# Attention weights turned by VectorE blocks and DMA instead of TensorE, weighted sums one head later, scores in two PSUM pools

## The chip, the cores and the metric

The kernel runs on one core of one Trainium2 chip. The metric is the device time of one execution in microseconds. Three runs of the kernel before took 1411.1, 1411.3 and 1412.79 us; the median is 1411.3 us. TensorE multiplies matrices into PSUM (eight banks here: three for projections, five for everything else), VectorE and ScalarE do elementwise work, reductions and activations, GpSimd some elementwise work, and SyncE issues nearly all DMAs on one queue, in order.

## The reference

One step of a two-layer encoder trunk in fp32, on 512 prompt tokens and 32 sample tokens of width 1024. Layer 0 mixes tokens by RWKV-7 and is not touched. Layer 1 is differential attention with 12 heads of width 128 (each query and key split into two halves of 64), beside four memory heads; everything is multiplied by a SiLU gate, projected out and added to the input.

```python
mask = k_pos[None, :] < (q_pos[:, None] // CHUNK + 1) * CHUNK
def probs(qa, ka):
    s = jnp.einsum('bqhd,bkhd->bhqk', qa, ka).astype(jnp.float32) * DF_HD ** -0.5
    return jax.nn.softmax(jnp.where(mask, s, NEG_INF), axis=-1)
attn = probs(q1, k1) - lam * probs(q2, k2)
return jnp.einsum('bhqk,bkhd->bqhd', attn.astype(v_all.dtype), v_all)
...
o = rmsnorm(o, subln) * (1.0 - lam_init)
out = jnp.concatenate([o.reshape(B, T, MIX_W), y_mem], axis=-1) * jax.nn.silu(gate)
```

The keys and values of layer 1 are outputs too (512 prompt and 32 sample rows, 12 heads).

## The kernel before

**Projections.** Activations lie transposed in SBUF, 128 features by 544 tokens, eight such tiles, each split into a high and a low part (hh, hl). A projection of 128 columns (gemm, line 341, called by proj, line 357) is 2 halves of 272 tokens × 8 tiles × 3 products = 48 matmuls into a PSUM tile called ps_g. Its weights come as two DMAs of 256 KB into raw (load, line 274), and ScalarE and VectorE split them into whi and wlo (split, line 303). There are five raw tiles and two pairs whi/wlo; used (line 293) splits the next block and issues the load of a later one.

**Layer 1** (layer1, line 1649) runs diff_group (line 1734) for three groups of four heads. For each head it projects v, k and q. The helper turned (line 1768) transposes v and k in 32×32 blocks on VectorE (tile kv) and writes them with four DMAs in runs of 128 bytes to a DRAM tile scr, from which vt (values by token) is read back and, at the end of the group, the outputs are copied. The high parts of k lie on half of the partitions of kh; a DMA kh<-kh copies each half to the other partitions, so that scores of both halves can be made with a correction kz.

**Attention of a head** is a loop over four query tiles t of 128 tokens, with n = 128 (t + 1) keys. For both maps, two matmuls give the scores in a PSUM tile ps_s of pool psc, which has two banks; VectorE sets the masked corner and takes the row maximum, ScalarE takes the exponential with its sum (softmax, line 1080), and VectorE forms the difference of both maps in pt (combine, line 1882). TensorE transposes the n columns of pt into ps_aT (pool psm, two banks), ScalarE copies them to aT, TensorE multiplies with vt into ps_o (pool psx, one bank), VectorE copies to ot and ScalarE takes the sum of squares.

**End of a group.** The same is done once for the sample tokens of four heads (tiles ssb, ps_saT, ps_os, os, ps_osT). Then rsqrt (line 124, nine small VectorE steps) gives the norms; for each head four scalings of ot, four transposes into ps_oT, a gate projection (gate, line 952, into one of two tiles sg) and two VectorE products into og follow. Groups 0 and 1 are followed by two memory heads each. In group 2, four of the sixteen og tiles are split ahead (early). After it comes the output projection (w_out, line 1226), which takes the heads of group 2 last.

**What sets the order.** In layer 1 nothing is ordered by hand. When the program is built, each engine's instructions are put in a fixed order: among those that the builder reckons ready, the one that stands first in the source goes first. On the chip each engine takes its instructions in that order and waits where one isn't ready. So TensorE's scores stand between matmuls of the next head's projections, and DMAs stand in SyncE's queue in the order that the builder reckoned.

Line 105 in the profile is the helper that issues every recorded operation, so rows are told apart by tile names.

Of the kernel before, what the change touches and what calls it, by code (L numbers as in the profile page):

```python
# [9 lines left out]
F32 = mybir.dt.float32  # L10
# [23 lines left out]
QB, KB, KVB = 2, 1, 2  # L34
# [73 lines left out]
class Trunk:  # L108
# [823 lines left out]
    def gate_evac(self, n):  # L932
        nc = self.nc
        sg = self.sg[n % SGB]

        def evac(ps, v):
            self.ae.activation(sg[:, v], ps, AF.Tanh, scale=0.5)
            gated = lambda: self.ve.scalar_tensor_tensor(sg[:, v], sg[:, v], 1.0, ps, ALU.add, ALU.mult)
            if not self.ordered:
                return gated()  # L940
            done.append(self.put_off(gated, 0.43))
            return gated

        done = []

        def get():
            self.until(done[-1])
            return sg

        return sg, get, evac  # L950

    def gate(self, src, c0):

        self.gates += 1
        sg, _, evac = self.gate_evac(self.gates)
        self.proj(src, c0, evac)
        return sg
# [136 lines left out]
    def mem_head(self, i, h, w, cq, cg, p):  # L1094

        st = {}
        it = self.mem_steps(st, i, h, p)
        for _ in range(3):
            next(it)
        st["q"], evac = self.query_evac(p)  # L1100
        self.proj(w, cq + h * P, evac)
        for _ in range(9):
            next(it)
        sg = self.gate(w, cg + h * P)
        st["gate"] = lambda: sg
        for _ in it:
            pass
# [207 lines left out]
    def layer0(self, mem):  # L1315
# [6 lines left out]
        with ExitStack() as ctx:  # L1322
# [45 lines left out]
            def add_gate(pr, st, c0, n):  # L1368
                def make(wt):
                    sg, st["gate"], evac = self.gate_evac(n)  # L1370
# [278 lines left out]
    def layer1(self):  # L1649
# [4 lines left out]
        with ExitStack() as ctx:  # L1654
            made, order = {}, list(range(8)) + [12, 13, 14, 15, 8, 9, 10, 11]
            with ExitStack() as c2:
# [9 lines left out]
                early = None  # L1666
                for hg in range(3):
                    self.diff_group(hg, w, p, self.ls[:, 2:3], early)
# [9 lines left out]
        with ExitStack() as ctx:  # L1678
# [36 lines left out]
            def consume(k, ps, v):  # L1715
                x = self.x1[:, k, v]
                self.ve.tensor_tensor(x, ps, x, ALU.add)
                self.square_sums((k, x, v), p, sums)
                if k == 3 and v.start:
# [14 lines left out]
    def diff_group(self, hg, w, p, nlam, early):  # L1734
# [9 lines left out]
        vs = p.tile([TS, 4, P], F32, tag="vs", name="vs")  # L1744
        scr = [self.dp.tile([T, 4, P], F32, tag=f"scr{i}", name=f"scr{i}", bufs=2) for i in range(2)]
        ssb = p.tile([P, 2, 160], F32, tag="ssb", name="ssb")
        on = []
        ss = p.tile([P, 3, 16], F32, tag="oss", name="oss")
        for j in range(4):
# [27 lines left out]
            vt = p.tile([P, 4, P], F32, tag="vt", name="vt", bufs=2)  # L1777
            self.se.dma_start(vt[:], scr[1][:TP, j, :].rearrange("(i p) d -> p i d", p=P))
# [6 lines left out]
            turned(0, k)  # L1785
            self.proj(w, h * P, q_parts)
            self.ae.copy(ks[:, j, :], k[:, TP:])
            if j == 1:
# [3 lines left out]
                self.ae.copy(ckT[:], ps[:].rearrange("p (j c) -> p j c", j=4))  # L1792
            if j == 3:
# [3 lines left out]
            ot = p.tile([P, 4, P], F32, tag="ot", name="ot", bufs=4)  # L1797
            on.append(ot)
# [23 lines left out]
        self.se.dma_start(vs[:], scr[1][TP:])  # L1822
# [9 lines left out]
        aT = p.tile([P, 512], F32, tag="aT", name="aTs", bufs=2)  # L1832
# [7 lines left out]
        for j in range(4):  # L1840
            rj = slice(32 * j, 32 * j + 32)
            self.te.matmul(po[rj, :P], aT[:TS, P + 32 * j : P + 32 * j + 32], vs[:, j, :], start=False, stop=True,
# [4 lines left out]
        jk = p.tile([P, P], F32, tag="jk", name="jks", bufs=2)  # L1847
# [7 lines left out]
        self.ae.activation(oT[:], psT[:, :P], AF.Copy, scale=self.subs)  # L1855
        self.ve.tensor_scalar(ss[:, 1, :], ss[:, 0, :], 1.0 / P, EPS, ALU.mult, ALU.add)
        self.rsqrt(ss[:, 2, :], ss[:, 1, :], p, "nt16")
        for j in range(4):
# [8 lines left out]
            self.ve.tensor_tensor(g[:, TP:], oT[:, 32 * j : 32 * j + 32], sg[:, TP:], ALU.mult)  # L1867

# [20 lines left out]
    def run(self):  # L1889
# [18 lines left out]
        self.sg, self.gates = [gp.tile([P, T], F32, name=f"sg{i}") for i in range(SGB)], 0  # L1908
# [54 lines left out]
```

## Time and profile before

| | |
|---|---|
| median of three runs | 1411.3 us |
| profiled execution, its own time | 1410.51 us |
| its span | 1408.8 us |
| granted TensorE clock, mean | 0.993 |
| busy: TensorE, weight loads | 1357.8, 1286.3 us |
| busy: VectorE, ScalarE, GpSimd | 915.3, 810.5, 423.3 us |
| DMA: packets, data | 315734, 151.07 MB |

Every row of a view names the source line, the engine (PE is TensorE, PEld its weight loads, DVE VectorE, ACT ScalarE, POOL GpSimd, SPq SyncE's queue), the operation, and output<-inputs by tile name with buffer numbers left out. In a group, "x120 | 21.3, 276 | 0.7" means 120 instructions, 21.3 us busy, 276 ns mean, and 0.7 us of idle time of that engine ahead of them, with what ended it. In a timeline a row gives start, duration and the number of instructions merged. Matmuls overlap, so a duration of 0.29 us can go with a start every 0.126 us. A row of waits reads: who waited <- for whom: total us, times, longest.

### The profile page before, as it was taken

What the parts mean: (1) busy time and instruction counts of PE and PEld (TensorE: products, weight loads), DVE (VectorE), ACT (ScalarE), POOL (GpSimd) and SP (SyncE); (2) the same over time, 40 slices, a digit from 0 to 9 for tenths busy, and PEclk for the clock granted to TensorE, in tenths of its full rate; (3) what the DMA queues carried; (4) which work ended last, traced back from release to release, by engine and by line L of the source; (5) the groups of instructions that cost most, each with busy time, mean ns of one, the idle gap of its engine ahead of it and who ended that gap; (6) DMA issues with size and microseconds to landing.
All of it is one profiled execution on the core that took longest, in us unless ns stands there. A gap on an engine that the chain in (4) does not pass through costs nothing.

```text
span 1408.8 us, 31764 instructions
## 1 busy us (share of the span) xinstructions
PE 1357.8 (96%) x11762; PEld 1286.3 (91%) x11762; DVE 915.3 (65%) x2352; ACT 810.5 (58%) x2239; POOL 423.3 (30%) x874
## 2 busy tenths in 40 slices
PE   6998999999999999899999999999999999999997
PEld 6998889999999999798899999999999999999996
DVE  7765777787778787665754566674465746568443
ACT  7665677767777777565533366554465445555321
POOL 2226576566856586520120040000001001110000
PEclk9999999999999999999999999999999999999998
DMA  7542223333233222333464474452444424453321
GB/s 241 176 136 59 62 62 83 84 75 78 63 84 90 68 65 75 90 89 105 136 191 126 139 216 109 100 157 83 114 99 112 145 75 103 102 140 119 105 68 64
DMA packets 315734, 151.07 MB, mean 107 GB/s; under 512 B 112361, under 2 KB 300018, under 8 KB 315578
## 3 DMA queue, kind: packets, MB, share of 16 engines
q1 hardware_dynamic: 315434, 148.50, 38.2%
q8 instruction: 93, 1.52, 0.4%
q14 instruction: 63, 0.52, 0.1%
q10 hardware_dynamic: 144, 0.52, 0.1%
HBM read 120.62 MB, written 31.69 MB: 108 GB/s over the span
## 4 chain that ended last, share of the span: by engine, by line
PE 45%; DVE 2%; ACT 1%; DMA 1%; issue 1%; DVEq 0%; ACTq 0%
PE ps_g L105 36%; PE ps_o L105 2%; PE ps_s L105 2%; PE ps_aT L105 1%; DVE wlo L105 1%; PE ps_mm L105 1%; DVE qp L105 1%; DMA kh<-kh 1%; PE ps_mo L105 1%; ACT whi L105 1%; PE ps_oT L105 0%; PE ps_mt L105 0%; ACT pt L105 0%; PE ps_f L105 0%; DVE snm L105 0%
## 5 line engine op out<-in xcount | busy, mean ns | idle before, releaser
L105 PE MATMUL ps_g<-hh,whi 128*128 128x272 f32 x1808 | 540.3, 299 | 0.9 <-ACT hh L105 0.9
L105 PE MATMUL ps_g<-hh,wlo 128*128 128x272 f32 x1808 | 539.2, 298 | 1.2 <-DVE wlo L105 1.2
L105 PE MATMUL ps_g<-hl,whi 128*128 128x272 f32 x1808 | 533.3, 295 | 0.6 <-POOL hl L477 0.5
L105 PEld LDWEIGHTS ps_g<-hh,whi 128*128 128x128 f32 x1808 | 343.7, 190 | 6.2 <-ACT hh L105 1.3
L105 PEld LDWEIGHTS ps_g<-hh,wlo 128*128 128x128 f32 x1808 | 343.1, 190 | 5.1 <-DVE wlo L105 2.0
L105 PEld LDWEIGHTS ps_g<-hl,whi 128*128 128x128 f32 x1808 | 342.9, 190 | 3.5 <-POOL hl L477 0.7
L105 DVE TENSOR_TENSOR wlo<-raw,whi 128x512 fp32r<-128x512 f32 x322 | 228.8, 722 | 165.8 <-ACT whi L105 164.0
L105 ACT CAST whi<-raw 128x512 fp32r<-128x512 f32 x322 | 194.5, 617 | 158.9 <-PE ps_g L105 129.6
L766 POOL TENSOR_TENSOR tm<-u,m 102x84 f32<-102x84 f32 (+23 forms) x372 | 154.6, 415 | 167.3 <-DMA m<-sc 139.1
L768 POOL TENSOR_TENSOR u<-u,tm 102x84 f32<-102x84 f32 (+23 forms) x372 | 162.9, 438 | 29.1
L105 PE MATMUL ps_g<-lo,whi 128*128 128x272 f32 x512 | 147.9, 289 | 0.7 <-DVE lo L105 0.7
L105 PE MATMUL ps_g<-hi,wlo 128*128 128x272 f32 x512 | 147.8, 289 | 0.0
L105 PE MATMUL ps_g<-hi,whi 128*128 128x272 f32 x512 | 147.7, 288 | 0.0
L1784 POOL TENSOR_TENSOR kz<-k,kh 64x544 fp32r<-64x544 f32 x24 | 37.0, 1540 | 318.8 <-ACT kh L105 317.9
L105 PEld LDWEIGHTS ps_g<-lo,whi 128*128 128x128 f32 x512 | 96.5, 188 | 1.1 <-DVE lo L105 1.1
L105 PEld LDWEIGHTS ps_g<-hi,whi 128*128 128x128 f32 x512 | 96.6, 189 | 0.0
L105 PEld LDWEIGHTS ps_g<-hi,wlo 128*128 128x128 f32 x512 | 96.5, 189 | 0.0
L105 DVE SCALAR_TENSOR_TENSOR SB<-ps_c,dl,sd 64x64 f32<-64x64 f32 x168 | 47.4, 282 | 44.0 <-PE ps_c L105 38.2
L105 ACT COPY sv<-ps_c 64x64 f32<-64x64 f32 x192 | 39.2, 204 | 38.2 <-PE ps_c L105 36.4
L105 ACT ACTIVATE pt<-ps_s,snm 128x128 f32<-128x128 f32 (+3 forms) x96 | 50.9, 531 | 15.0 <-DVE snm L105 14.2
L105 ACT ACTIVATE sg<-ps_g 128x272 f32<-128x272 f32 x64 | 25.2, 394 | 42.4 <-PE ps_g L105 40.0
L105 DVE TENSOR_REDUCE snm<-ps_s 128x1 f32<-128x128 f32 (+3 forms) x96 | 46.1, 485 | 1.0
(367 smaller groups left out, 2496.1 us busy)
## 6 DMA issues: line engine op xcount, KB each, us to landing
raw<-in_rw_in_dram SPq DMA_DIRECT2D x114, 256.0 KB
raw<-in_df_in_dram SPq DMA_DIRECT2D x112, 256.0 KB
raw<-in_w_out_dram SPq DMA_DIRECT2D x64, 256.0 KB
scr<-kv SPq DMA_DIRECT2D x96, 68.0 KB
out_dram<-scr SPq DMA_DIRECT2D x6, 1024.0 KB
m<-sc SPq DMA_DIRECT2D x36, 128.0 KB
oscr<-sg SPq DMA_DIRECT2D x16, 272.0 KB
lo<-oscr SPq DMA_DIRECT2D x16, 272.0 KB
```

Source lines behind the costliest of these rows:

```text
L105: return lambda *a, **k: self.trunk.tie(self, issue(*a, **k))
L766: nc.gpsimd.tensor_tensor(tm[:, :n, :wd], u3[:, :n, kx : kx + 1].to_broadcast(sh), m3[:, kx : kx + 1, kx + 1 :].to_broadcast(sh), ALU.mult)
L768: nc.gpsimd.tensor_tensor(u3[:, :n, kx + 1 :], u3[:, :n, kx + 1 :], tm[:, :n, :wd], ALU.add)
L1784: nc.gpsimd.tensor_tensor(kz[rows[m], m, :], k[rows[m], :], hi.bitcast(F32), ALU.subtract)
```

## The change

The attention weights are no longer transposed on TensorE. After combine, VectorE transposes pt in 32×32 blocks into a tile pk, which holds all ten 128×128 parts of a head (40 × 32 columns; one buffer). When the head's four query tiles are done, four DMAs write pk in runs of 128 bytes to a DRAM tile ptr (two buffers). The read of ptr into aT, now one tile for all ten parts (one buffer), stands in the source behind the next head's q projection. The weighted sums of all four query tiles stand behind the next head's softmax; they go into the four quarters of one PSUM bank, with one copy to ot and then four sums of squares. For the fourth head of a group, the read stands behind the second of the four gate projections and the sums behind the fourth.

The four gate projections of a group now stand together ahead of the norms, and each writes into its head's tile og, in which the product is formed in place. The two sg tiles serve as the buffers of turned. Scores of query tiles 1 and 3 go to pool psm, those of 0 and 2 to psc. The read of vt stands behind the writes of k. The copies of keys and values to the outputs (kv_out) move from the end of a group to the third head of the next, and for the last group into the output projection. The new rows of the sample's values use ck's buffer.

```diff
+        def weighted(j, ptr, vt):
+            aT = p.tile([P, 10, P], F32, tag="aT", name="aT", bufs=1)
+            self.se.dma_start(aT[:], ptr[:].rearrange("(i b) t c -> (b t) i c", b=4))
+            yield
+            ot = p.tile([P, 4, P], F32, tag="ot", name="ot", bufs=4)
+            on.append(ot)
+            po = self.psx.tile([P, 4, P], F32, tag="x", name="ps_o")
+            for t in range(4):
+                i0 = t * (t + 1) // 2
+                for i in range(t + 1):
+                    self.te.matmul(po[:, t, :], aT[:, i0 + i, :], vt[:, i, :], start=i == 0, stop=i == t)
+            self.ve.tensor_copy(ot[:], po[:])
+            for t in range(4):
+                jk = p.tile([P, P], F32, tag="jk", name="jk", bufs=1)
+                self.ae.activation(jk[:], ot[:, t, :], AF.Square, accum_out=ss[:, 0, 4 * j + t : 4 * j + t + 1])
...
             def turned(i, x):
-                kv = p.tile([P, T // 32, 32], F32, tag="kv", name="kv", bufs=KVB)
-                self.ve.transpose(kv[:].rearrange("p b c -> p (b c)"), x[:])
+                kv = self.sg[i][:].rearrange("p (b c) -> p b c", c=32)
+                self.ve.transpose(self.sg[i][:], x[:])
...
             turned(1, v)
-            vt = p.tile([P, 4, P], F32, tag="vt", name="vt", bufs=2)
-            self.se.dma_start(vt[:], scr[1][:TP, j, :].rearrange("(i p) d -> p i d", p=P))
...
             turned(0, k)
+            vt = p.tile([P, 4, P], F32, tag="vt", name="vt", bufs=2)
+            self.se.dma_start(vt[:], scr[1][:TP, j, :].rearrange("(i p) d -> p i d", p=P))
             self.proj(w, h * P, q_parts)
+            if late:
+                next(late)
...
+            if j == 2:
+                before()
...
-                    ps = self.psc.tile([P, 512], F32, tag="c", name="ps_s")
+                    q, g = (self.psm, "m") if t % 2 else (self.psc, "c")
+                    ps = q.tile([P, 512], F32, tag=g, name="ps_s")
...
                 self.combine(pt, rs, n, nlam)
-                ps = self.psm.tile([P, 512], F32, tag="m", name="ps_aT")
-                for i in range(t + 1):
-                    self.te.transpose(ps[:, i * P : i * P + P], pt[:, 0, i * P : i * P + P], self.ident[:])
-                aT = p.tile([P, 512], F32, tag="aT", name="aT", bufs=2)
-                self.ae.copy(aT[:, :n], ps[:, :n])
-                po = self.psx.tile([P, 512], F32, tag="x", name="ps_o")
-                for i in range(t + 1):
-                    self.te.matmul(po[:, :P], aT[:, i * P : i * P + P], vt[:, i, :], start=i == 0, stop=i == t)
-                self.ve.tensor_copy(ot[:, t, :], po[:, :P])
-                jk = p.tile([P, P], F32, tag="jk", name="jk", bufs=2)
-                self.ae.activation(jk[:], ot[:, t, :], AF.Square, accum_out=ss[:, 0, 4 * j + t : 4 * j + t + 1])
+                b0 = 2 * t * (t + 1)
+                self.ve.transpose(pk[:, b0 : b0 + 4 * (t + 1)].rearrange("p b c -> p (b c)"), pt[:, 0, :n])
+            if late:
+                next(late, None)
+            ptr = self.dp.tile([40, 32, P], F32, tag="ptr", name="ptr", bufs=2)
+            for b in range(4):
+                self.se.dma_start(ptr[:, :, 32 * b : 32 * b + 32].rearrange("n t c -> t n c"), pk[32 * b : 32 * b + 32])
+            late = weighted(j, ptr, vt)
...
-        for i in range(2):
-            self.se.dma_start(o[4 + i][0, 0, :, 4 * hg : 4 * hg + 4, :], scr[i][:TP])
-            self.se.dma_start(o[10 + i][0, 0, :, 4 * hg : 4 * hg + 4, :], scr[i][TP:])
+        def kv_out():
+            for i in range(2):
+                self.se.dma_start(o[4 + i][0, 0, :, 4 * hg : 4 * hg + 4, :], scr[i][:TP])
+                self.se.dma_start(o[10 + i][0, 0, :, 4 * hg : 4 * hg + 4, :], scr[i][TP:])
...
+        sgs = []
+        for i, g in enumerate(range(4 * hg, 4 * hg + 4)):
+            sgs.append(self.gate(w, 3 * MIXW + 512 + g * P, g))
+            if i == 1:
+                next(late)
+        next(late, None)
         self.ve.tensor_scalar(ss[:, 1, :], ss[:, 0, :], 1.0 / P, EPS, ALU.mult, ALU.add)
...
-            sg = self.gate(w, 3 * MIXW + 512 + (4 * hg + j) * P)
-            g = self.dest(4 * hg + j, sg)
+            g = sg = sgs[j]
```

More of the change, by code (lines that the diff above doesn't have):

```diff
@@ L33 @@
 KAPPA = 0.5 * math.exp(-0.5)
-QB, KB, KVB = 2, 1, 2
+QB, KB, PKB = 2, 1, 1
 RKV = 4
@@ L950, in gate_evac, with gate @@
         return sg, get, evac
-    def gate(self, src, c0):
-        self.gates += 1
-        sg, _, evac = self.gate_evac(self.gates)
+    def gate(self, src, c0, g):
+        sg, _, evac = self.gate_evac(self.o1[g])
         self.proj(src, c0, evac)
@@ L1103, in mem_head @@
             next(it)
-        sg = self.gate(w, cg + h * P)
+        sg = self.gate(w, cg + h * P, 12 + h)
         st["gate"] = lambda: sg
@@ L1666, in layer1 @@
                 early = None
+                kv_out = lambda: None
                 for hg in range(3):
-                    self.diff_group(hg, w, p, self.ls[:, 2:3], early)
+                    kv_out = self.diff_group(hg, w, p, self.ls[:, 2:3], early, kv_out)
                     for h in ((0, 1), (2, 3), ())[hg]:
@@ L1718, in consume @@
                 self.square_sums((k, x, v), p, sums)
+                if k == 2 and not v.start:
+                    kv_out()
                 if k == 3 and v.start:
@@ L1732, in layer1, with diff_group @@
                 pass
-    def diff_group(self, hg, w, p, nlam, early):
+    def diff_group(self, hg, w, p, nlam, early, before):
         nc, a, o = self.nc, self.a, self.o
@@ L1743, in diff_group @@
         ks = p.tile([P, 4, TS], F32, tag="ks", name="ks")
-        vs = p.tile([TS, 4, P], F32, tag="vs", name="vs")
         scr = [self.dp.tile([T, 4, P], F32, tag=f"scr{i}", name=f"scr{i}", bufs=2) for i in range(2)]
         ssb = p.tile([P, 2, 160], F32, tag="ssb", name="ssb")
-        on = []
+        on, late = [], None
+        def weighted(j, ptr, vt):
[13 more added lines that the diff above has]
+                self.ae.activation(jk[:], ot[:, t, :], AF.Square, accum_out=ss[:, 0, 4 * j + t : 4 * j + t + 1])
         ss = p.tile([P, 3, 16], F32, tag="oss", name="oss")
@@ L1841, in diff_group @@
             rj = slice(32 * j, 32 * j + 32)
-            self.te.matmul(po[rj, :P], aT[:TS, P + 32 * j : P + 32 * j + 32], vs[:, j, :], start=False, stop=True,
+            self.te.matmul(po[rj, :P], aT[:TS, P + 32 * j : P + 32 * j + 32], vs[:TS, j, :], start=False, stop=True,
                              tile_position=(0, 32 * j))
@@ L1907, in run @@
         gp = self.pool("gate", 1)
-        self.sg, self.gates = [gp.tile([P, T], F32, name=f"sg{i}") for i in range(SGB)], 0
+        self.sg = [gp.tile([P, T], F32, name=f"sg{i}") for i in range(SGB)]
         self.rctx = ExitStack()
```

16 lines of the change are left out of this document (8 added, 8 removed).

## The prediction

> **What bounds the kernel now.** I read the page first (engines, chain), then the busy time of the stage that the change touches, then TensorE's own waits in it, and last the order of instructions around one head.
>
> ```profile
> span 1408.8 us, 31764 instructions
> PE 1357.8 (96%) x11762; PEld 1286.3 (91%) x11762; DVE 915.3 (65%) x2352; ACT 810.5 (58%) x2239; POOL 423.3 (30%) x874
> PE 45%; DVE 2%; ACT 1%; DMA 1%; issue 1%; DVEq 0%; ACTq 0%
> ```
>
> The page: TensorE is busy nearly throughout and has by far the largest share of the chain that ended last. The change lies in the differential attention, from 833 us (first DMA of a turned head) to 1283 us. The table of stretches (columns: PE, PEld, DVE, ACT, POOL busy, granted clock, DMA share, GB/s) and TensorE's waits there:
>
> ```profile
> 833.00:1283.00 450.00, 444.37 (x3415) 417.38 (x3415) 267.65 (x793) 241.59 (x715) 40.62 (x26) 1.00 0.43 115
> 858.00:861.00 3.00, 3.00 (x25) 2.91 (x26) 1.86 (x5) 0.79 (x3) 0.00 (x0) 1.00 0.98 231
> 861.00:866.00 5.00, 5.00 (x41) 4.80 (x40) 1.42 (x3) 2.77 (x7) 0.00 (x0) 1.00 0.14 22
> PE ps_s L105 <- ACT pt L105: 3.5, 7, 0.6
> PE ps_s L105 <- DMA kh<-kh: 0.6, 2, 0.3
> ```
>
> TensorE is busy 444.4 of 450 us, and its two kinds of wait shown are 3.5 and 0.6 us in total; VectorE is at 59%, ScalarE at 54%, the DMA engines at 43%. While a softmax runs, TensorE multiplies the next head's projection, so this stage lasts as long as TensorE's instructions take. Whatever leaves TensorE there comes off the time, as long as no new wait appears. Because matmuls overlap, their durations say too much; I price by the distance between starts.
>
> **The change part by part.**
>
> *The transposes of the weights leave TensorE* (10 per head, 120 in all, in runs of 1 to 4). One run in order of time, with the projection's matmuls (ps_g) around it, and the plain rate of ps_g from the chain:
>
> ```profile
> 860.34 0.29 PE L105 MATMUL ps_g<-hl,whi 128*128 128x272 f32 x1
> 860.53 0.63 PE L105 MATMUL ps_aT<-ident,pt 128*128 128x128 f32 x4
> 860.91 0.37 PE L105 MATMUL ps_g<-hh,wlo 128*128 128x272 f32 x1
> 861.12 0.29 PE L105 MATMUL ps_g<-hh,whi 128*128 128x272 f32 x1
> ...
> 889.12 7.42 PE ps_g L105 x59
> ```
>
> 59 matmuls in 7.42 us are 0.126 each. From the start of the ps_g ahead of the run to the start of the second ps_g behind it, less these two: 861.12 − 860.34 − 2 × 0.126 = 0.53 us for four, 0.13 each with the switch between kinds of matmul inside. I take shorter runs in proportion: 1.33 us a head, **15.9 us** in all.
>
> *The weighted sums stay, but in one run per head instead of four.* They appear as two passes each:
>
> ```profile
> 854.65 0.28 PE L105 MATMUL ps_g<-hl,whi 128*128 128x272 f32 x1
> 854.89 0.71 PE L105 MATMUL ps_o<-vt,aT 128*128 128x128 f32 x4
> 855.36 0.37 PE L105 MATMUL ps_g<-hh,wlo 128*128 128x272 f32 x1
> 855.57 0.29 PE L105 MATMUL ps_g<-hh,whi 128*128 128x272 f32 x1
> ...
> 861.62 0.29 PE L105 MATMUL ps_g<-hl,whi 128*128 128x272 f32 x1
> 861.89 1.16 PE L105 MATMUL ps_o<-vt,aT 128*128 128x128 f32 x8
> 862.80 0.37 PE L105 MATMUL ps_g<-hh,wlo 128*128 128x272 f32 x1
> 863.01 0.29 PE L105 MATMUL ps_g<-hh,whi 128*128 128x272 f32 x1
> ```
>
> Four passes cost 0.92 − 0.25 = 0.67 us, eight 1.39 − 0.25 = 1.14: 0.118 a pass and 0.20 per run. Three runs fewer per head save 0.6 us, **7.2 us** in all; at worst (each 0.20 is a wait for aT that comes back in another form) nothing.
>
> *Scores in two pools.* The 3.5 us of ps_s on the exponentials above are the wait for one of two score banks. With four banks I take them as gone: **3.5 us**, between 0 and 3.5. Four banks may also join score matmuls into fewer runs; at 0.20 per run, as for ps_o, that is up to 48 × 0.2 = 9.6 us more, of which I count none.
>
> *What the new path puts on VectorE and ScalarE.* Rows by form in this stage:
>
> ```profile
> L105 DVE COPY ot<-ps_o 128x128 f32<-128x128 f32 x48 | 13.9, 289 | 30.8 <-PE ps_o L105 30.6
> L105 DVE STREAM_TRANSPOSE kv<-k 128x544 f32<-128x544 f32 x12 | 8.9, 738 | 0.0
> L105 DVE TENSOR_SCALAR ot<-ot,oss 128x128 f32<-128x128 f32 x32 | 7.7, 281 | 0.0
> ```
>
> Block transposes: 1280 columns per head at 738/544 = 1.36 ns are 1.74 us, 20.8 us in all. Out go the 13.9 us of ot copies; in come 12 wider ones (at most four old ones, 1.16 us each). So VectorE gets 7 to 21 us more on 267.65 of 450, ScalarE loses its copies of aT. Neither sets the end: VectorE's share stays under 70%, so both fit under TensorE's matmuls. A block transpose needs pk free, that is the last head's writes landed; behind it on VectorE stand the next softmax and the splits of weights (wlo) that TensorE needs. A head lies between, so I price this at nothing. VectorE also stops waiting 30.6 us for ps_o in the middle of its queue, which lets a softmax end up to 2.5 us earlier.
>
> *What it puts on the DMA engines.* Per head four writes with 40 × 32 × 4 = 5120 runs of 128 bytes and one read with 1280 runs of 512 bytes. Two looks at the DMA queue, 858 to 862 us and 884 to 888 us, have different mixes:
>
> ```profile
> DMA packets 3296, 0.80 MB, mean 201 GB/s; under 512 B 2272, under 2 KB 3296, under 8 KB 3296
> q1 hardware_dynamic: 3296, 0.80, 90.4%
> ...
> DMA packets 2887, 0.60 MB, mean 150 GB/s; under 512 B 2256, under 2 KB 2887, under 8 KB 2887
> q1 hardware_dynamic: 2887, 0.60, 73.0%
> ```
>
> In engine time: 2272 s + 1024 b = 0.904 × 64 us = 57.9 and 2256 s + 631 b = 46.7, so b = 28 ns and s = 13 ns. The writes are 5120 × 13/16 = 4.2 us of all engines, the read 2.2: 6.4 per head, 77 us in all on 0.43 × 450 = 194. A share of about 63% still fits. The traffic moved later (the copies of k and v to the outputs) is the same amount.
>
> *Two new places where TensorE can wait.* All of this goes on SyncE's one queue, in order:
>
> ```profile
> 858.41 2.33 SPq L105 DMA_DIRECT2D scr<-kv  x4
> 865.59 0.39 SPq L105 DMA_DIRECT2D raw<-in_df_in_dram  x1
> 866.22 1.13 SPq L105 DMA_DIRECT2D kh<-kh  x2
> 867.52 0.45 SPq L105 DMA_DIRECT2D vt<-scr  x1
> ...
> 866.22 4.73 DMA kh<-kh
> ```
>
> The writes wait for the last block transpose, the read waits for the writes and for the last head's ps_o; behind them in the queue stand the raw loads and kh<-kh. First, the read of aT, which ps_o waits for. Its nearest relative is vt, read back from what scr<-kv wrote. In the source vt stands ahead of the k projection; in the fixed order it was put behind kh, which needs the whole k projection. The writes had left the queue by 861 us (share 0.14 from then on), so that order reckons with a round trip of 6 us or more where the chip took about 3. An order that is too careful places ps_o after aT is there. I take 0 us; one microsecond too early per head makes 12, and the next head's v projection stands behind it.
>
> Second, kh<-kh, the swap that the next head's scores need. It is in the chain with 4.73 us and has no margin: the second of the wait rows above shows TensorE already waiting for it. A softmax of head 0 is over at 860.5 (its transposes start at 860.53), kh goes out at 866.22: 5.7 us. TensorE's savings take 2.1 us from this gap, the last block transpose 0.7, the quicker softmax gives back up to 2.5; so 2.9 to 5.4 us for a burst of 4.2. The wait is 0 to 1.3 us for each of 11 heads; I take 0.3, what the longest such wait measures now: **+3.3 us**.
>
> *Gates, sample path, tail.* The four gates are the same matmuls into other tiles, and stand now as cover over the sample's softmax. Behind them come the last head's sums, 16 scalings (16 × 0.281 = 4.5 us) and the squares and small steps ahead of them; I put this at 11 us. Cover: the memory heads after groups 0 and 1; after group 2 the output projection's six part products that don't need these heads, 144 × 0.126 = 18 us. Cost 0 to 3 us, once; I take **+1**. Without that cover it would be 11.
>
> Sum: −15.9 − 7.2 − 3.5 + 3.3 + 1.0 = −22.3 us. The profiled execution took 1410.5 us (its span 1408.8 and 1.7 around it) and would take 1388.2; it stands 0.8 under the median of 1411.3, so against the median the forecast is **1389 us**. Bounds: with no new wait −26.6 (1385); with sums in one run worth nothing, score waits unchanged, kh at 1.3 us a head and the tail at 3: −15.9 + 14.3 + 3 = +1.4 (1413).
>
> **The rivals.**
>
> *The swap stands behind the weights (slower).* If the four writes go out right ahead of kh<-kh, what is left of the 4.2 us burst delays every head's scores, and TensorE, which takes its instructions in order, waits. It decides at 26.6/11 = 2.4 us a head, more than half the burst. With three quarters left (3.2 us): 1411.3 − 26.6 + 35 = 1420. For it: no margin for kh, a queue at 98% during such writes. Against: the gap of 2.9 to 5.4 us.
>
> *Sums too early.* ps_o is put where aT isn't there yet, 1 us per head: 1389 + 12 = 1401. For it: two DRAM trips in a row, one aT buffer. Against: the place of vt.
>
> *No change.* Savings and waits cancel, for instance because weights (raw) queue behind 77 us more of DMA: 1411. Against: no row in which TensorE waits for raw.
>
> *Scattered writes are far dearer than scr's.* In a stage of 428 us, with 194 us of other traffic and 26 of reads, 208 us stay for 61,440 runs, 3840 per engine: 54 ns each, four times the 13 measured. At six times, 300 us, the stage lasts 520 and the kernel 1389 + 92 = 1481. Packets of the same form in scr<-kv speak against it. The Trainium skill ("VectorE: DVE Perf Modes", The three transpose paths) warns that a plain DMA copy doing a transpose by strides is 19× slower than the crossbar one, and its table for kernel authors sends a 128×128 transpose to TensorE. By that rule this change would be a loss; the trace disagrees for this shape, since the blocks are turned on VectorE and runs of 128 bytes stay whole at 13 ns.
>
> **How the numbers follow.** Forecast (1384 to 1396): 0.54. Better than that, by score matmuls in fewer runs (about 1381): 0.10. Sums too early or half the gain eaten (about 1401): 0.14. No change: 0.07. Swap behind the weights: 0.13. Dear writes: 0.02. The range 1380 to 1410 leaves out the last two cases, part of no change and little of the better one. A measurement of this kernel tells 0.2%, 2.8 us, from no change: faster 0.78, same 0.07, slower 0.15.
>
> **What would show it.** Right: no ps_aT, TensorE's starts as dense as now, ps_o in runs of 20 passes, the stage some 22 us shorter (450 to 428), rows of TensorE waiting for aT or kh under 5 us. Wrong: a row "PE ps_s <- DMA kh" or "PEld ps_o <- DMA aT" with more than 1 us a head, ps_g's starts spread by late weights, or a hole at the start of the output projection.

## The result and the profile after

The changed kernel takes 1474.3 us (median of four runs, 1473.3 to 1476.9) against 1411.2 us before (four runs): ratio 1.045, 95% interval 1.043 to 1.047. It is 63 us slower where 22 us less were forecast. The page of the changed kernel, its first two lines, and its table of stretches (columns as in the prediction), first changed, then before:

```profile
span 1473.0 us, 31439 instructions
PE 1374.1 (93%) x11642; PEld 1298.4 (88%) x11642; DVE 938.0 (64%) x2364; ACT 794.0 (54%) x2191; POOL 425.2 (29%) x874
```

```profile
833.00:1360.00 527.00, 472.80 (x3445) 443.12 (x3444) 298.58 (x845) 233.22 (x686) 41.53 (x27) 0.93 0.55 132
```

```profile
833.00:1360.00 527.00, 521.37 (x4031) 493.95 (x4031) 311.54 (x900) 268.48 (x770) 40.84 (x27) 1.00 0.42 112
```

TensorE has 120 matmul records fewer in all, yet it does only 3445 in this stretch instead of 4031: the stretches are equally long, and the changed kernel is not as far at the end of its own. TensorE idles, and the clock that it is granted falls to 0.93. No other engine is full: VectorE 298.6 of 527, DMA share 0.55. The largest of TensorE's waits from 833 us to the end, changed kernel:

```profile
PE ps_g L105 <- ACT whi L105: 19.3, 9, 2.9
PE ps_oT L105 <- DVE ot L105: 19.0, 10, 5.8
PE ps_s L105 <- ACT pt L105: 4.3, 8, 1.3
PE ps_g L105 <- DVE wlo L105: 3.8, 6, 1.0
```

All rows of that view add up to 55.4 us, against 5.6 before. The lower clock, counted over the time from 833 us to the end in which TensorE is busy, costs another 34 us (an estimate from the trace's clock records), against nothing before. So 50 + 34 us came in; the span grew by 64.2, so some 20 us of TensorE's work are gone: about the predicted saving, under a loss of about 84. There is no row of TensorE waiting for kh or for aT, the two waits that the prediction priced.

Where the waits come from is seen around the second head. SyncE's waits from 833 to 1360 us, its queue in order of time, and then ScalarE's, TensorE's and again ScalarE's rows and the stretches there:

```profile
SPq L105 <- DVE pk L105: 100.9, 8, 19.0
SPq L105 <- DVE wlo L105: 96.0, 29, 11.1
```

```profile
865.17 1.11 SPq L105 DMA_DIRECT2D kh<-kh  x2
...
875.54 1.74 SPq L105 DMA_DIRECT2D scr<-sg  x2
895.60 2.40 SPq L105 DMA_DIRECT2D ptr<-pk  x4
898.05 1.49 SPq L105 DMA_DIRECT2D scr<-sg  x2
899.63 1.02 SPq L105 DMA_DIRECT2D raw<-in_df_in_dram  x2
900.76 1.11 SPq L105 DMA_DIRECT2D kh<-kh  x2
```

```profile
879.47 1.32 ACT L105 CAST kh<-k 64x544 fp32r<-64x544 f32 x2
```

```profile
882.10 0.22 PE L105 MATMUL ps_s<-kh,qp 128*128 128x128 f32 x1
...
890.81 0.39 PE L105 MATMUL ps_g<-hh,whi 128*128 128x272 f32 x1 [2.87 <-ACT whi L105]
```

```profile
889.48 0.68 ACT L105 ACTIVATE pt<-ps_s,snm 128x512 f32<-128x512 f32 x1
...
890.14 0.61 ACT L105 CAST whi<-raw 128x512 fp32r<-128x512 f32 x1
```

```profile
882.00:887.90 5.90, 5.80 (x41) 5.22 (x39) 4.88 (x25) 2.98 (x12) 1.50 (x1) 1.00 0.01 3
887.90:890.80 2.90, 0.03 (x1) 0.00 (x0) 2.87 (x9) 2.59 (x8) 0.00 (x0) 1.00 0.00 0
890.80:900.00 9.20, 8.22 (x54) 8.01 (x55) 7.63 (x15) 4.42 (x15) 0.00 (x0) 0.81 0.49 75
```

And TensorE's first scores of that head in the kernel before:

```profile
871.09 0.30 PE L105 MATMUL ps_s<-kh,qp 128*128 128x128 f32 x1 [0.32 <-DMA kh<-kh]
```

From 877.3 (875.54 + 1.74) to 895.6 the four writes of ptr stand at the head of SyncE's queue and wait for the last block transpose of the second head, which ends at 895.57 and stands behind that head's softmax. Behind them wait half the writes of v, two raw loads and the third head's kh<-kh, whose input is ready at 880.79 (the casts above) and which goes out 20 us later; from 882.0 to 890.8 the DMA engines do next to nothing (share 0.01 and 0.00). On the other side, the softmax is late because TensorE's scores are: kh<-kh went out at 865.17, a microsecond earlier than before the change, and yet the scores start at 882.10, eleven microseconds later than before. TensorE's fixed order has them there, behind 122 matmuls of the next projections that follow ps_ckT; before the change they follow it at once. When they come, eight exponentials stand ahead of the cast of whi on ScalarE, TensorE runs out of weights (2.87 us), and in the 9 us behind that it is granted 0.81 of its clock.

### The profile page after: what moved, and what is told of

The parts are those of the page before. It is cut to its first block, busy times and chain, and to the rows that moved or that the text cites. A ratio compares the mean times of both kernels' runs of the same rounds, so it can differ in the third digit from the quotient of the medians.

```text
span 1473.0 us, 31439 instructions
## 1 busy us (share of the span) xinstructions
PE 1374.1 (93%) x11642; PEld 1298.4 (88%) x11642; DVE 938.0 (64%) x2364; ACT 794.0 (54%) x2191; POOL 425.2 (29%) x874
## 5 line engine op out<-in xcount | busy, mean ns | idle before, releaser
L105 PE MATMUL ps_g<-hh,whi 128*128 128x272 f32 x1808 | 538.9, 298 | 20.3 <-ACT whi L105 19.3
L105 DVE TENSOR_TENSOR wlo<-raw,whi 128x512 fp32r<-128x512 f32 x322 | 231.9, 734 | 181.6 <-ACT whi L105 178.9
L105 ACT COPY raw<-ps_g 128x272 f32<-128x272 f32 x74 | 28.4, 386 | 30.4 <-PE ps_g L105 29.7
```

What stands on the lines that cost most here:

```text
L105: return lambda *a, **k: self.trunk.tie(self, issue(*a, **k))
```

## The experiments

Each is timed against the kernel before in the same set of runs; the ratio is to that kernel, with its 95% interval.

**The parts beside the turned path.** *e1_pools*: the kernel before, scores of t = 1 and 3 in psm.

```diff
-                    ps = self.psc.tile([P, 512], F32, tag="c", name="ps_s")
+                    q, g = (self.psm, "m") if t % 2 else (self.psc, "c")
+                    ps = q.tile([P, 512], F32, tag=g, name="ps_s")
```

> The kernel before with one edit: scores of query tiles 1 and 3 in the other pool, four banks instead of two. Nothing else. Theory A (order: the loss of the change comes from the fixed order of instructions, which was made for DMA writes reckoned longer than they are), theory B (traffic: the 128-byte writes themselves hold up other transfers on the chip) and theory C (tail: the gates moved together leave TensorE without cover at the end of each group) all expect the term of the prediction: 3.5 us less than 1411, so 1408, down to 1401 if score matmuls join into fewer runs. A time above 1412 would say that the pools themselves cost something.

1415.1 us, 1.0025 (1.0015 to 1.0035): 3.8 us lost where 3.5 were to be gained.

*e2_tail*: the changed kernel with the old attention body (transposes on TensorE, sums at once, one score pool); the gates in place, the sg tiles for turned, vt and kv_out stay moved.

```diff
-                self.ve.transpose(pk[:, b0 : b0 + 4 * (t + 1)].rearrange("p b c -> p (b c)"), pt[:, 0, :n])
+                for i in range(t + 1):
+                    self.te.transpose(ps[:, i * P : i * P + P], pt[:, 0, i * P : i * P + P], self.ident[:])
...
```

> The changed kernel without the new path of the weights and without the second score pool: TensorE transposes and the sums follow at once as before; kept are the four gates together and in place, sg tiles as buffers, vt and the outputs of k and v later. Theory C expects most of the loss here: three waits of about 6 us for the scaled sums, a lower clock behind them, 1430 or more. Theories A and B expect 1411 within 5 us, since there is no write of weights.

1408.4 us, 0.9985 (0.9974 to 0.9996). The tail and the gates cost nothing.

*e3_pe_turn*: the whole change, except that TensorE turns the weights, into one tile per head; no pk by VectorE, no ptr.

```diff
-                self.ve.transpose(pk[:, b0 : b0 + 4 * (t + 1)].rearrange("p b c -> p (b c)"), pt[:, 0, :n])
...
+                    self.te.transpose(ps[:, i * P : i * P + P], pt[:, 0, i * P : i * P + P], self.ident[:])
...
+                self.ae.copy(pk[:, i0 : i0 + t + 1], ps[:, :n].rearrange("p (i c) -> p i c", c=P))
...
-            for b in range(4):
-                self.se.dma_start(ptr[:, :, 32 * b : 32 * b + 32].rearrange("n t c -> t n c"), pk[32 * b : 32 * b + 32])
```

> The changed kernel with one step undone: the weights are transposed by TensorE and copied by ScalarE into one tile of ten parts; the sums still follow one head later in one bank, gates and pools as changed. Theories A and B expect 1411 less 7 (sums in one run) less 3.5 (pools): 1400, range 1395 to 1408. Theory C expects 1430 or more.

1414.0 us, 1.0016 (1.0003 to 1.0029). So 60 of the 63 us are lost on the path of block transposes, writes and read. Sums in one run and two pools together gain nothing here: e3 takes 5.7 us more than e2, which has neither.

**The swap ahead of the writes.** *e5_after_swap*: the writes stand behind the next head's kh<-kh, those of the fourth head behind the first gate.

```diff
...
+            send()
             turned(0, k)
...
-            for b in range(4):
-                self.se.dma_start(ptr[:, :, 32 * b : 32 * b + 32].rearrange("n t c -> t n c"), pk[32 * b : 32 * b + 32])
+            def send(ptr=ptr, pk=pk):
+                for b in range(4):
+                    self.se.dma_start(ptr[:, :, 32 * b : 32 * b + 32].rearrange("n t c -> t n c"), pk[32 * b : 32 * b + 32])
...
```

> The changed kernel with the same operations and the same DMA traffic; only the place of the four writes of weights moves, from the end of a head's softmax to behind the next head's swap kh<-kh (for the fourth head behind the first gate). The planned order then has a head's scores directly behind its q projection again. Theory A expects most of the loss back: 1385 to 1405. Theory B expects 1450 or more, since every write is still there. Theory C expects 1440 or more, because the gates stand as in the changed kernel.

1506.5 us, 1.067 (1.065 to 1.069): worse, though the scores of the second head now stand 16 projection matmuls behind ps_ckT and no row of SyncE waiting for pk is left. The theory that the swap alone is held up fell. The order did not become good everywhere, so this run is no clean test of it: in the first group the third and fourth heads' first scores start 13.0 and 12.9 us after their kh<-kh goes out, against 10.8 and 7.1 in the changed kernel.

**Buffer, order or traffic.** *e7_pk2*: two buffers of pk; to make room, the squares of ot are written over ps_o and some small sample tiles share other buffers (also in the other runs with two buffers).

```diff
-QB, KB, PKB = 2, 1, 1
+QB, KB, PKB = 2, 1, 2
...
```

> The changed kernel with two buffers for pk instead of one (room for it: the squares of ot are written over ps_o instead of jk, and the small sample tiles share the buffers of ck and ckT). TensorE's fixed order is the same as in the changed kernel up to one place at the end of a group. Three theories for the loss of 63 us. Buffer theory (the block transposes wait until the last head's writes have left the single pk, and the exponentials, the splits of weights and TensorE stand behind them): 1410 to 1440, and the row of ScalarE's pt waiting for VectorE's pk gone. Order theory (the fixed order puts the second head's scores some 100 matmuls too late, so the softmax, the writes and the weight loads behind them bunch up, whatever the chip does): 1460 to 1478. Traffic theory (61,440 runs of 128 bytes slow all other loads): 1465 to 1478.

1475.8 us, 1.044 (1.041 to 1.047): no difference. *e8_whole*: ptr written and read in whole runs; it leaves out putting the blocks in place, so its sums are not those of the reference.

```diff
...
-                self.se.dma_start(ptr[:, :, 32 * b : 32 * b + 32].rearrange("n t c -> t n c"), pk[32 * b : 32 * b + 32])
+                self.se.dma_start(ptr[32 * b : 32 * b + 32, :], pk[32 * b : 32 * b + 32].rearrange("p b c -> p (b c)"))
```

> The changed kernel with ptr written and read in whole runs of 5120 bytes (the same 640 KB each way, 128 runs instead of 5120 and 1280; the 32x32 blocks are then not put in place, so the sums take weights that are turned within blocks only). TensorE's fixed order is nearly the same as in the changed kernel: the second head's scores stand behind 79 instead of 122 projection matmuls. Traffic theory: the small runs were the cost, so 1395 to 1415. Order theory: the scores still stand too late, 1445 to 1475. Buffer theory: pk is free some 4 us earlier per head, 1420 to 1455.

1457.1 us, 1.031 (1.029 to 1.033). Without a single small run in ptr, 45 of the 63 us are still lost, which is in the range of the order theory and 2 us above that of the buffer theory, and SyncE's wait is still there:

```profile
SPq L105 <- DVE pk L105: 96.1, 8, 16.6
```

*e9_traffic*: e3 with the small writes added on GpSimd's queue; nobody reads them.

```diff
...
+            for b in range(4):
+                nc.gpsimd.dma_start(ptr[:, :, 32 * b : 32 * b + 32].rearrange("n t c -> t n c"), pk[32 * b : 32 * b + 32].rearrange("p i (a c) -> p (i a) c", c=32))
```

> The variant with the weights turned by TensorE (1414.0 us), with the four writes of 5120 runs of 128 bytes per head added: from its tile of turned weights to DRAM, on GpSimd's queue, read by nobody and waited for by nobody but the tile's next use two heads later. TensorE's fixed order stays that of the variant but for two runs of sums. Traffic theory: 1440 to 1475, since 61,440 small runs slow the weight loads and the swap. Order and buffer theories: 1412 to 1424.

1413.3 us, 1.001 (0.9996 to 1.0023), as e3. 61,440 runs of 128 bytes cost nothing that these runs can tell when nobody stands behind them: the traffic theory fell. *e6_direct*: sixteen DMAs per head from pk to aT, no ptr.

```diff
...
+                for a in range(4):
+                    self.se.dma_start(aT[32 * b : 32 * b + 32, :, 32 * a : 32 * a + 32], pk[32 * a : 32 * a + 32, b::4, :])
```

> The changed kernel without the DRAM trip: sixteen DMAs per head put the 32x32 blocks of pk straight into place in aT (SBUF to SBUF, runs of 128 bytes, no read back, no ptr); with one buffer of aT they start when the last head's sums are done. The fixed order puts the second head's scores behind 121 projection matmuls, like the changed kernel's. Traffic theory: a third less DMA time (no reads of 1280 runs per head), 1440 to 1460. Order theory: 1455 to 1490. Buffer theory: pk now stays taken until the sums of the head before are done, so 1470 to 1500.

1488.9 us, 1.054 (1.052 to 1.056), in the ranges of the order and the buffer theory: a trip less, but more DMAs on the same queue, which now wait for the last head's sums too (TensorE waits 14.8 us for aT). It does not tell the two theories apart.

**The queue.** *q_act*: writes and read on ScalarE's queue. *q_pool*: both on GpSimd's. *q_pool2*: the latter with two buffers of pk.

```diff
-            self.se.dma_start(aT[:], ptr[:].rearrange("(i b) t c -> (b t) i c", b=4))
+            nc.scalar.dma_start(aT[:], ptr[:].rearrange("(i b) t c -> (b t) i c", b=4))
...
-                self.se.dma_start(ptr[:, :, 32 * b : 32 * b + 32].rearrange("n t c -> t n c"), pk[32 * b : 32 * b + 32])
+                nc.scalar.dma_start(ptr[:, :, 32 * b : 32 * b + 32].rearrange("n t c -> t n c"), pk[32 * b : 32 * b + 32])
```

> The changed kernel with the four writes of ptr and the read of aT issued on ScalarE's queue instead of SyncE's; nothing else is edited. Queue theory (on SyncE's queue the writes of a head wait up to 19 us for its last block transpose, 100.9 us in all, and the raw loads and the next head's kh<-kh that stand behind them wait too; so one head's softmax, writes, swap and the next softmax become one serial chain): this chain is cut, 1395 to 1425, and TensorE's wait for whi (19.3 us) falls below 5. Order theory (sums and scores stand at bad places in TensorE's fixed order whatever the queue): 1440 or more.

1425.6 us, 1.010 (1.008 to 1.012): 49 us of the loss are gone, and so are the row of SyncE waiting for pk and TensorE's row of waits for whi; the time is at the upper bound of the queue theory's range.

> As the run before, with the writes of ptr and the read of aT on GpSimd's queue. Queue theory: 1395 to 1425, a little more than on ScalarE's queue where GpSimd's kz waits behind a write. Order theory: 1440 or more.

1450.1 us, 1.027 (1.024 to 1.029), in the order theory's range: SyncE's queue is free of the writes here, and yet TensorE has 16.9 us of ps_oT waiting for ot at the end of a group and 9.4 us for aT.

> As the run before, with two buffers of pk (the small tiles share buffers as in e7_pk2). Queue theory: within 10 us of the run before, since two buffers alone gave nothing. If with the queue freed the single pk becomes the next wait: 10 to 25 us below it.

1438.0 us, 1.018 (1.016 to 1.021): with the queue freed the second buffer is worth 12 us. *e10_swap_pk2* is e5 with two buffers of pk (the diff is that of e5 and of e7_pk2).

> The variant with the writes behind the next head's swap (1506.5 us), with two buffers of pk. In that variant the block transposes stood late in VectorE's fixed order because pk was reckoned taken by writes that are issued a head later, and the exponentials stood behind them. Buffer theory for that variant: 1400 to 1440. Queue theory: kh<-kh is no longer behind the writes, but raw loads still are, 1460 to 1510.

1470.8 us, 1.041 (1.039 to 1.043): 36 us less than e5, so the buffer mattered there, and still 59 over before, in the queue theory's range. But SyncE waits only 0.7 us for pk in it. TensorE's waits are spread over many causes, and the order is late again; its largest wait, and the third head's kh<-kh and first scores:

```profile
PE ps_sc L105 <- ACT qs L105: 8.9, 3, 3.0
```

```profile
892.13 1.19 SPq L105 DMA_DIRECT2D kh<-kh  x2
904.27 0.23 PE L105 MATMUL ps_s<-kh,qp 128*128 128x128 f32 x1
```

The scores stand 12.1 us behind their swap.

**What was left.** *e11_last_pe*: q_act, with the last head of each group turned by TensorE and its sums behind the first gate.

```diff
...
+                if j < 3:
+                    self.ve.transpose(pk[:, b0 : b0 + 4 * (t + 1)].rearrange("p b c -> p (b c)"), pt[:, 0, :n])
+                else:
...
+                    for i in range(t + 1):
+                        self.te.transpose(ps[:, i * P : i * P + P], pt[:, 0, i * P : i * P + P], self.ident[:])
+                    self.ae.copy(pk[:, b0 : b0 + 4 * (t + 1)].rearrange("p b c -> p (b c)"), ps[:, :n])
...
```

> The variant with ptr on ScalarE's queue (1425.6 us), and the last head of each group turned by TensorE into pk, its sums made without a DRAM trip behind the first gate projection. The other nine heads stay on the new path. If the rest of the loss is the group's end (last sums late, TensorE waiting for ps_oT's input, half clock behind it): 1400 to 1412. If it is the waits for aT between the scores (8.5 us) and the 4 us of ScalarE per head for issuing: 1418 to 1426.

1421.6 us, 1.008 (1.006 to 1.010): the range of the waits for aT and of ScalarE's issuing, so the group's end is not the rest. *e12_last_pk2*: the same with two buffers of pk.

> As the run before with two buffers of pk (small tiles share buffers as in e7_pk2). If the single pk buffer holds up the exponentials once the queue is free (34.5 us of ScalarE waiting for pk): 5 to 15 us under the run before; otherwise within 3 us of it.

1422.0 us, 1.009 (1.007 to 1.011): no difference. *e14_wpool_rpool*: e11 on GpSimd's queue.

> As e11, with writes and read on GpSimd's queue instead of ScalarE's. If ScalarE's issuing is the rest: 1395 to 1405. If the waits for aT are: at or above e11. The same queue with all heads on the new path took 1450.

1416.6 us, 1.004 (1.002 to 1.006): under e11, and above the range for ScalarE's issuing; aT is still waited for (9.9 us). *e15_wact_rsp*: e11 with the read of aT back on SyncE's queue.

```diff
-            nc.scalar.dma_start(aT[:], ptr[:].rearrange("(i b) t c -> (b t) i c", b=4))
+            self.se.dma_start(aT[:], ptr[:].rearrange("(i b) t c -> (b t) i c", b=4))
```

> As e11, with the writes on ScalarE's queue and the read of aT on SyncE's. TensorE's fixed order then has the sums in one run some 44 projection matmuls behind the next head's scores instead of between them. If the waits for aT are the rest: 1395 to 1408, and no row of TensorE waiting for aT. If the group's end alone was: as e11.

1401.8 us, 0.993 (0.992 to 0.995): faster than before, with no row of TensorE waiting for aT. *e16_wact_all*: the changed kernel and nothing but the four writes on ScalarE's queue; all heads on the new path.

```diff
-                self.se.dma_start(ptr[:, :, 32 * b : 32 * b + 32].rearrange("n t c -> t n c"), pk[32 * b : 32 * b + 32])
+                nc.scalar.dma_start(ptr[:, :, 32 * b : 32 * b + 32].rearrange("n t c -> t n c"), pk[32 * b : 32 * b + 32])
```

> The changed kernel with one edit: the four writes of ptr on ScalarE's queue; the read of aT stays on SyncE's. Queue theory with sums early as second cause: TensorE's fixed order has the sums some 44 matmuls behind the next head's scores, so no wait for aT; with all twelve heads on the new path 1397 to 1410 if the end of the group costs little, 1410 to 1420 if the last head's sums still come late for ps_oT.

1403.3 us, 0.994 (0.992 to 0.996): one edit turns 1474 into 1403, 9 us (0.6%) faster than before. Its queues around the second head (SyncE, then ScalarE), TensorE's first scores of the second and third heads, the stretch, and TensorE's largest waits:

```profile
866.08 1.14 SPq L105 DMA_DIRECT2D kh<-kh  x2
867.26 2.47 SPq L105 DMA_DIRECT2D scr<-sg  x3
869.83 1.02 SPq L105 DMA_DIRECT2D raw<-in_df_in_dram  x2
870.91 0.51 SPq L105 DMA_DIRECT2D aT<-ptr  x1
...
890.75 1.27 SPq L105 DMA_DIRECT2D kh<-kh  x2
```

```profile
860.28 4.19 ACTq L1838 DMA_DIRECT2D ptr<-pk  x4
864.52 0.39 ACT L105 COPY k<-ps_g 128x272 f32<-128x272 f32 x1 [3.78 <-DMA ptr<-pk]
```

```profile
870.66 0.22 PE L105 MATMUL ps_s<-kh,qp 128*128 128x128 f32 x1
...
895.41 0.23 PE L105 MATMUL ps_s<-kh,qp 128*128 128x128 f32 x1
```

```profile
833.00:1360.00 527.00, 510.59 (x3976) 491.28 (x3975) 334.39 (x915) 250.23 (x725) 38.46 (x27) 0.99 0.59 144
```

```profile
PE ps_sc L105 <- ACT qs L105: 6.1, 3, 2.1
PE ps_oT L105 <- DVE ot L105: 2.5, 5, 0.7
PE ps_g L105 <- DVE qp L105: 2.3, 4, 1.2
```

The third head's kh<-kh goes out at 890.75 instead of 900.76, the second head's scores start at 870.66 instead of 882.10, the third head's 4.7 us after its swap instead of 10.8, and the clock is 0.99. ScalarE copies nothing in the 4 us in which it issues the writes: k waits 3.78 us in the row above. Whether the waits that stay come from that is not shown; the largest, 6.1 us for qs, was 8.9 us in e10, where SyncE issues the writes. *e17_one_pool*: e15 with one score pool (the edit of e1 the other way round).

> e15 with all scores in one pool of two banks, as before the change. If two pools cost here what they cost alone in e1 (3.7 us over no change): 1396 to 1400. If they are a gain on the new path, where no transposes use the other pool: 1404 to 1410.

1417.9 us, 1.005 (1.003 to 1.007): on the new path two pools are worth 16 us, more than the range on record for a gain; without them TensorE's wait for the swap grows from 1.3 us in e15 to:

```profile
PE ps_s L105 <- DMA kh<-kh: 9.2, 5, 3.1
```

**What stays open.** Moving the writes off the queue does two things at once: nothing waits behind them on the chip, and the fixed order of the other engines, which is made with the queue in mind, changes (28 instead of 122 matmuls between ps_ckT and the scores). That the two together cost about 71 us is shown by e16. How they share it is not. In e10 neither the swap nor a wait for pk holds up the queue, its scores stand 12 us behind their swap, and 59 us are still lost: there a loss of that size comes about without the writes' wait at the head of the queue. In q_pool the queue is free of the writes too, the scores of the second to fourth heads start 4.5 to 6.4 us after their swap, and 38 us are lost all the same. But no run had the free queue with the changed kernel's order, or the other way round. An order of TensorE written out by hand over the changed kernel's queue was not tried.

## Why the prediction was wrong

*The transposes off TensorE (−15.9).* Right as far as the runs reach. With the queue mended, e16 is 10.7 us faster than e3, where TensorE turns the weights, and pays more for waits (16.1 us of rows against 11.0) and clock (0.99 against 1.00 over 527 us, some 5 us): an estimate of 21 for this term, which includes whatever else differs between the two orders.

*Sums in one run (−7.2) and scores in two pools (−3.5).* Wrong as terms. One head's sums in e16:

```profile
879.84 0.29 PE L105 MATMUL ps_g<-hh,whi 128*128 128x272 f32 x1
879.96 2.39 PE L105 MATMUL ps_o<-vt,aT 128*128 128x128 f32 x20
882.11 0.37 PE L105 MATMUL ps_g<-hl,whi 128*128 128x272 f32 x1
882.32 0.29 PE L105 MATMUL ps_g<-hh,wlo 128*128 128x272 f32 x1
```

Twenty passes take 2.48 − 0.25 = 2.23 us, a little less than the 2.56 of the prediction's two prices. So in that kernel the run is as cheap as priced, but e3, which has both edits, took 1414.0 where these terms give some 1402: with transposes on TensorE the two together gained nothing, and the second, alone, lost 3.8 us (e1). A second pool is no term by itself: in e1 the scores take banks from the transposes, in e15 against e17 nobody else uses them and they are worth 16 us.

*kh<-kh (+3.3).* This is the step that failed. The queue was described rightly ("behind them in the queue stand the raw loads and kh<-kh") and then priced by the 4.2 us that the four writes were estimated to transfer. What the runs showed in its place: the first write of a head waits at the head of SyncE's queue for the last block transpose, up to 19.0 us and 100.9 us in all, and with the same four writes on ScalarE's queue the kernel is 71 us faster (e16). How much of this is the hold-up on the chip and how much the fixed order made around it stays open. The cost was also expected in the wrong row, a wait of TensorE for kh, which does not exist. It shows in the order: scores late, softmax late, whi and wlo behind the exponentials, ps_oT behind the sums. Of the prediction's signs of being wrong, the one that appeared is ps_g spread by late weights (19.3 us for whi, 3.8 for wlo). The prediction knew from vt that the order reckons with longer DMA trips than the chip takes, and applied it only to the sums; e16 shows that the place of the scores changes with the writes' queue too (28 matmuls behind ps_ckT instead of 122).

*aT (0).* Right, and read the wrong way. The order is careful, as argued from vt: no wait for aT. But a sum that stands too late is late for others; at a group's end ps_oT waited up to 5.8 us for ot (19.0 us in all). With the last head's sums early, this row fell from 16.9 us in q_pool to 2.3 in e14. In q_act, with the read on ScalarE's queue, the sums stand between the scores and wait 8.5 us for aT: the rival "sums too early", in another kernel.

*VectorE (under 70%).* Right: 298.6 of 527 changed, 334.4 in e16. In e16 the four block transposes of a head take 301 + 428 + 568 + 704 ns = 2.0 us, where 1.74 were worked out:

```profile
L105 DVE STREAM_TRANSPOSE pk<-pt 128x512 f32<-128x512 f32 x12 | 8.5, 704 | 0.1
L105 DVE STREAM_TRANSPOSE pk<-pt 128x384 f32<-128x384 f32 x12 | 6.8, 568 | 0.0
L105 DVE STREAM_TRANSPOSE pk<-pt 128x256 f32<-128x256 f32 x12 | 5.1, 428 | 0.0
L105 DVE STREAM_TRANSPOSE pk<-pt 128x128 f32<-128x128 f32 x12 | 3.6, 301 | 0.0
```

The single pk, priced at nothing, is worth nothing in the changed kernel (e7), 12 us with the writes on GpSimd's queue (q_pool2) and 36 in e5.

*DMA engines (63%).* Right: 0.59 in e16's stretch, and in e9 the writes cost nothing that can be told. The rival "dear writes" named 1481, near the result, for a cause that e9 excludes; e8 leaves at most 17 us for small runs, by queue and order included.

*Gates, sample path, tail (+1).* Small, as forecast, though with the other sign: e2 is 2.9 us faster than before.

*The clock.* It was not in the sum at all. Beside 50 us of added waits, the changed kernel lost some 34 us by the clock that was granted around them.

*The rival "swap behind the weights"* had the place in the queue and the sign, with a chance of 0.13, but not the mechanism: no row of the changed kernel has TensorE waiting for kh. Its 1420 came from the same mistake, a burst of 4.2 us instead of a wait of up to 19. The range, 1380 to 1410, could not hold the time: no bound was taken for a queue whose head waits for something other than DMA.

## What to carry to other kernels

For each DMA that a change puts on a shared queue, ask what its input waits for and for how long, and count that time for everything behind it; the transfer may be the smallest part. A DMA that waits for late work belongs on a queue where little that is urgent stands behind it, here ScalarE's for the writes but not for the read, which made 71 us and 22 us of difference with the same bytes moved (the fixed order changed with the queue each time). Where an order is fixed ahead by reckoned times, a new long step can show up as work in the wrong place on other engines, not as a wait for the step.

## What the runs showed of the hardware

The engine that issues a DMA is no side matter: with four writes a head on ScalarE's queue instead of SyncE's, and the order that came with it, the kernel is 71 us faster. The Trainium skill ("DMA: Bandwidth & Descriptors", Issuing engines are not separate DMA queues) says that starting DMAs from several engines saves only the time to start them, usually small. By that, e16 would gain at most the time that SyncE takes to start the writes, 2.4 to 4.1 us a head and 32 us over twelve heads in the changed kernel (an estimate); it gains more. The same page (Anatomy of one DMA — SWDGE (gpsimd) path) says, of a path that SyncE does not use but of DMA engines in general, that waiting for a semaphore happens on the issuing sequencer before dispatch. The trace of SyncE's queue agrees: it waits 100.9 us for pk, and in one such wait the third head's kh<-kh, ready at 880.79, goes out at 900.76, with a DMA share of 0.01 and 0.00 from 882.0 to 890.8. How much of the 71 us is this and how much the order is not shown.

TensorE's clock fell behind short idle times. In q_act two waits of 1.40 and 1.41 us that ended 2.15 us apart were followed by 10 us at about half clock (TensorE's rows, then the stretches):

```profile
1261.80 0.37 PE L105 MATMUL ps_g<-hh,whi 128*128 128x272 f32 x1 [1.40 <-DVE qp L105]
1263.95 0.55 PE L105 MATMUL ps_s<-kh,qp 128*128 128x256 f32 x1 [1.41 <-DMA kh<-kh]
```

```profile
1264.00:1274.00 10.00, 9.40 (x53) 8.61 (x54) 3.02 (x17) 2.86 (x13) 0.00 (x0) 0.51 0.89 266
1274.00:1280.00 6.00, 6.00 (x51) 5.96 (x50) 5.86 (x20) 4.16 (x13) 0.00 (x0) 1.00 0.00 0
```

The Trainium skill ("TensorE: Matmul & The Clock Gate", Why this matters for your kernels) advises to have no idle gap of TensorE over about 3 us. Here two idle times that add up to 2.8 us were followed by half clock, so gaps shorter than that can cost too. Not every wait did: in the stretch of the kernel before, waits of up to 0.6 us left the clock at 1.00. Against the kernel before, 50 us of added waits went with some 34 us of lost clock in the changed kernel, 22 with 11 in q_act and 10 with 5 in e16 (estimates from the clock records, over TensorE's busy time).
